# A fifth raw weight tile, adding DMAs by row blocks, a mingled step order and squares in passing tiles, in a two-layer decoder trunk

## The chip, the cores and the metric

The kernel runs on one core of one Trainium2 chip. The metric is the device time of one launch in microseconds; the time before is the median of three runs. A profile of one execution is given beside the runs.

The engines are named as in the profile: PE is TensorE (matmul), PEld its weight loads, DVE VectorE, ACT ScalarE, POOL GpSimd, SP SyncE. L12 is line 12 of the kernel.

## What is computed

The reference is a decoder trunk of two layers, D = 2048, a sequence of 256 tokens, float32. Cut to what matters:

```python
for l in range(2):
    h = rms_norm(x, attn_norm[l])
    proj = h @ w_in[l]                    # (256, 6160): columns of two head groups
    o_gla = gated linear attention        # 8 heads, chunks of 64
    o_sb = stick-breaking attention       # 8 heads, blocks of 128
    x = x + concat(o_gla, o_sb) @ w_o[l]
    hm = rms_norm(x, mlp_norm[l])
    up = square(relu(hm @ w_up[l]))       # (256, 8192)
    x = x + up @ w_down[l]
```

The change touches the last part of each layer: a rest of the input projection, the output projection, and above all the two big products of the MLP, which read 64 MB of weights each and layer.

## The kernel before

**Precision by splitting.** A float32 operand is split into a high part (its rounding to the fast matmul format, copied by ACT) and a low part (the operand less its high part, by DVE). One product of two 128-row blocks is three matmuls, high x high, high x low and low x high (L1312 to L1314); the moving side is 512 columns of weights, the stationary side 128 x 128 activations. A weight block's parts are `whi` (ACT, L1209) and `wlo` (DVE, L1213).

**Units, pairs and steps.** After the attention, a layer is a list of units: one of the gate projection ("g"), two of the output projection ("o"), then for each quarter q of the hidden width two "up" and two "down" units (n2 = 0 and 1). An up or down unit multiplies all 256 tokens with a 2048 x 1024 block of weights. It does so in eight pairs, a pair being two blocks of 128 weight rows, 1024 columns wide: one raw tile of 1 MB, loaded by one DMA on SP's queue (`load`, L1188). Four of the pairs (`FAST`, 1, 3, 5, 6) go through a Strassen-like scheme with seven products in place of eight, for which DVE first makes sums of weight blocks (`ts` and in place in `raw`, L1066); they have four steps. The others have two steps. `STEPS` lists, step by step, which pair is next; a step makes one weight operand pair of parts and then its products, into the PSUM banks that `step_banks` names.

**Adding DMAs.** For pairs 2 and 7 (`ADDED`) DVE makes no low part. ACT writes the negated high part into a tile `dlo` (L1219), and a DMA issued by POOL (L1222) adds the raw weights onto it; its landing is what the second matmul of the product waits for. A step of such a pair takes one column half (512 columns) of both row blocks, so that the DMA's source has two pieces of 2 KB in each partition.

**Rings.** Raw tiles are a ring of four (`RAWS`): three in the pool `weights`, one (`raw2`) in the pool of the MLP. A load waits until everyone who reads the tile four loads back is done, DMAs included. High parts have a ring of five, low parts one of four, `dlo` one of two. Activations (`act`, 4 KB a partition) share 19 tiles; 2 KB tiles for passing values (`t2`) are five.

**Tails.** After an up unit's last products into each bank, DVE combines the banks (`up_tail`: L1066, tile `act`), ACT applies ReLU, PE transposes the result (L1419) at the start of the next unit, ACT squares it out of PSUM (L1427) into a tile `t` of the `act` ring, and `forms` makes the parts for the down units. A down unit's tail adds the banks to the residual `xb`. The next unit's first products need the banks that the tail reads.

**The order on the queues.** `Plan` simulates the units before they are emitted: every piece has an engine, a length and a lag. PE, SP and POOL keep their order as listed; for DVE and ACT the piece that is due first goes first. What comes out is each engine's program order, and an engine that waits for one instruction holds back all behind it. Two constants tell the plan how long a transfer takes to land: 4.6 us for a load, 7.0 us for an adding DMA.

Of the kernel before, what the change touches and what calls it, by code (L numbers as in the profile page):

```python
# [20 lines left out]
T2 = 5  # L21
STEPS = [0, 0, 1, 1, 1, 1, 2, 3, 3, 2, 3, 3, 4, 4, 5, 5, 5, 5, 6, 6, 6, 6, 7, 7]
FAST = (1, 3, 5, 6)
# [20 lines left out]
class Plan:  # L44
# [10 lines left out]
    class Piece:  # L55
        def __init__(self, engine, length, fn, deps, lag):
            self.engine, self.length, self.fn, self.lag = engine, length, fn, lag
            self.deps = deps
            self.users = []
            for d in deps:  # L60
                d.users.append(self)

# [9 lines left out]

    def run(self):
        t = 0.0
        for p in self.pieces:
            if p.engine == "PE":
                p.due = t
                t += p.length
        for p in reversed(self.pieces):
            if p.engine != "PE":  # L80
                p.due = min([u.due for u in p.users], default=t) - p.length - p.lag - self.GAP
# [50 lines left out]
def trunk_kernel(  # L132
# [27 lines left out]
    xpool = ctx.enter_context(tc.tile_pool(name="resid", bufs=1, side="right"))  # L160
    apool = ctx.enter_context(tc.tile_pool(name="acts", bufs=19))
    ppool = ctx.enter_context(tc.tile_pool(name="parts", bufs=4))
# [34 lines left out]
    def tmp(tag, shape, dt=F32, bufs=2):  # L197
        pool = pools["att"] if tag in ATT else pools["mlp"] if tag in MLP else tpool
        return pool.tile(list(shape), dt, tag=tag, name=nm(tag), bufs=bufs)
# [584 lines left out]
    for l in range(DEPTH):  # L784
# [277 lines left out]
        MM, TR, V2, V1, A2, A1 = 0.227, 0.108, 1.15, 0.61, 1.0, 0.55  # L1062
        RING, LOWS, ADDS, RAWS = 5, 4, 2, 4

# [19 lines left out]

        def step_banks(kind, is_fast):

            if kind == "g":
                return (1, 6), (1, 6)
            return ((2, 3), (5, 7), (1, 6), (4,)) if is_fast else ((2, 4), (3, 8))

# [84 lines left out]
        def load(u, i):  # L1175

            box = []
            x = len(raws)

            def fn():  # L1180
                if x % 4 == 0:
                    box.append(tmp("raw2", [P, 2, 1024], bufs=1))
                else:
                    box.append(wpool.tile([P, 2, 1024], F32, tag="raw", name=nm("raw")))
                dst = box[0]
                if units[u][0] == "g":
                    dst = dst.rearrange("p k (c n) -> p (k c) n", c=2)
                nc.sync.dma_start(dst, weights(u, i))  # L1188

            readers = []  # L1190
            piece = add("SP", 2.9, fn, raws[x - RAWS] if x >= RAWS else [], lag=4.6)
            raws.append(readers)
            return (lambda: box[0]), piece, readers

        def high_tile():
# [4 lines left out]
        def parts(src, readers, deps, n=2, by_dma=False):  # L1200
# [23 lines left out]
            if by_dma:  # L1224
                m = add("ACT", A2, negated, deps, dlo[-ADDS] if len(dlo) >= ADDS else [])
                lo = add("POOL", 2.7, add_weights, m, lag=7.0)
                dlo.append([])
                readers.extend((m, lo))
# [16 lines left out]
        def steps(u, j, is_fast, r, ld, readers):  # L1245
# [17 lines left out]
            def ext(i):  # L1263
                return lambda: (op.x[j][:, i, 0, :], op.x[j][:, i, 1, :])

            if not is_fast:
                for c, ms in ((0, (2, 4)), (1, (3, 8))):
                    sl = slice(c * 512, (c + 1) * 512)
                    yield parts(
                        lambda sl=sl: r()[:, :, sl], readers, ld,  # L1270
                        by_dma=kind in ("up", "down") and j in ADDED,
                    ), [(m, [(blk(k, tt), k) for k in range(2)]) for tt, m in enumerate(ms)]
                return
            def row(k):
                return r()[:, k, :].rearrange("p (c n) -> p c n", c=2)

# [90 lines left out]
        def up_tail(u):  # L1367
# [37 lines left out]
            def turn(h):  # L1405
# [3 lines left out]

                def new_t():  # L1410
                    box["t", h] = act_tile(F32, (P, 2, 2, T))

                for i, m in enumerate(((5, 7), (1, 6))[h]):
# [10 lines left out]
                    def square(i=i):  # L1424
                        if i == 0:
                            new_t()
                        nc.scalar.activation(  # L1427
                            box["t", h][:, i].rearrange("p j t -> p (j t)"),
                            box["p", h, i], AF.Square,
                        )  # L1430
# [7 lines left out]
                    done["down", q, pair] = made(  # L1438
                        lambda i=i, pair=pair: forms(op, pair, box["t", h][:, i], "sx"),
                        None, fast(pair), sq,  # L1440
# [111 lines left out]
        for u, (kind, q, n2) in enumerate(units):  # L1552
# [4 lines left out]
            for j in order:  # L1557
                uses.append(step_banks(kind, j in quick)[of_pair[j]])
                of_pair[j] += 1
            last_use = {m: k for k, ms in enumerate(uses) for m in ms}  # L1560
            begun, p, running = set(), {}, {}
            was = units[u - 1] if u else None
            for k, j in enumerate(order):
                if j not in running:
                    running[j] = steps(u, j, j in quick, *load(u, j))
                (box, h, lo, users), prods = next(running[j])
# [78 lines left out]
```

## Time and profile before

| | |
|---|---|
| runs | 2192.98, 2190.72, 2193.82 us; median 2192.98 |
| profiled execution | 2189.26 us, of which span 2187.5 |
| granted clock of PE | 1.0 |
| PE, DVE, ACT, POOL busy | 99%, 85%, 66%, 9% of the span |
| MB moved, mean rate | 476.16 MB, 218 GB/s |

The up and down units of the first layer run from about 412 us to 1094 us, those of the second from about 1501 us to the end; the attention parts lie before them. A row of a table of windows has the stretch, its length, then for each engine the busy time and the number of instructions, the granted clock, the share of the 16 DMA engines that is busy, and GB/s. A row of the waits has who waited, for whom, the sum in us, how often, and the longest. A row of the timeline has the start, the duration, engine, line, operation, tiles and, in brackets, the idle time before it and what ended it. A row of a tile or line has the duration in ns (least, median, most) and the first and last start. In rows of DMA queues stand packets, MB and the share of 16 engines; in rows of DMA issues the KB of each and the median us to landing.

### The profile page before, as it was taken

How to read it: one execution, taken by the hardware profiler on the slowest of the kernel's cores; microseconds unless marked ns; L12 is line 12 of the kernel's file. 1: busy time of each engine (PE TensorE's matmuls, PEld its weight loads, DVE VectorE, ACT ScalarE, POOL GpSimd, SP SyncE). 2: the span in 40 equal slices, each digit the busy share in tenths (PEclk: the TensorE clock that was granted, in tenths of full speed). 3: DMA queues.
4: the chain of work that ended last, by engine and by line, in shares of the span. 5: the costliest groups of instructions: out<-in, count | busy, mean ns of one | idle time of the engine just before them, and what ended most of it. 6: DMA issues, size and time to landing. Idle time of an engine off the chain costs nothing.

```text
span 2187.5 us, 28276 instructions
## 1 busy us (share of the span) xinstructions
PE 2162.9 (99%) x10256; PEld 1781.3 (81%) x10256; DVE 1852.4 (85%) x2469; ACT 1451.4 (66%) x1855; POOL 196.1 (9%) x202
## 2 busy tenths in 40 slices
PE   9999999999999999999999999999999999999999
PEld 7988778878888888788878887788778878888887
DVE  5777569999999989999957775699899999999898
ACT  5555356677677677677745553667776776776775
POOL 0020000011010101101100200000010111111010
PEclk9999999999999999999999999999999999999999
DMA  6645455678979988888856544557888889889887
GB/s 233 194 154 159 149 175 191 211 218 254 260 231 248 254 250 234 258 255 232 224 163 193 169 158 152 175 173 217 234 250 262 229 247 262 243 239 259 250 233 212
DMA packets 179184, 476.16 MB, mean 218 GB/s; under 512 B 8698, under 2 KB 33858, under 8 KB 179044
## 3 DMA queue, kind: packets, MB, share of 16 engines
q1 hardware_dynamic: 144228, 407.24, 55.5%
q0 software_dynamic: 34816, 67.12, 18.1%
q8 instruction: 80, 1.31, 0.2%
q14 instruction: 60, 0.49, 0.1%
HBM read 405.12 MB, written 2.10 MB: 186 GB/s over the span
## 4 chain that ended last, share of the span: by engine, by line
PE 67%; DMA 14%; DVE 11%; issue 5%; ACT 1%; POOL 1%; SPq 0%; DVEq 0%; POOLq 0%; ACTq 0%
DMA dlo<-raw 7%; PE acc L557 6%; PE acc L558 6%; PE acc L559 6%; DVE wlo L1213 5%; DMA raw<-in_w_up_dram 4%; PE acc L604 3%; DMA raw<-in_w_down_dram 2%; PE acc L608 1%; DVE ts L1066 1%; DVE act L1066 1%; DVE raw L1066 1%; DVE xb L1066 1%; ACT whi L1209 1%; POOL dlo L1222 1%
## 5 line engine op out<-in xcount | busy, mean ns | idle before, releaser
L1209 ACT ACTIVATE whi<-raw 128x1024 fp32r<-128x1024 f32 (+1 forms) x728 | 701.5, 976 | 296.2 <-DVE raw L1066 45.2
L1213 DVE TENSOR_TENSOR wlo<-raw,whi 128x1024 fp32r<-128x1024 f32 (+1 forms) x600 | 654.6, 1097 | 65.8 <-ACT whi L1209 53.9
L540 DVE TENSOR_TENSOR wlo<-raw,whi 128x1024 fp32r<-128x1024 f32 (+2 forms) x194 | 220.5, 1140 | 134.0 <-ACT whi L538 133.8
L538 ACT ACTIVATE whi<-raw 128x1024 fp32r<-128x1024 f32 (+2 forms) x194 | 189.8, 983 | 203.8 <-PE acc L559 154.2
L1222 POOL DMA_DIRECT2D dlo<-raw x128 | 154.7, 1267 | 1502.4 <-ACT dlo L1219 1211.1
L557 PE MATMUL acc<-whi,act 128*128 128x512 f32 (+2 forms) x640 | 242.3, 379 | 0.0
L558 PE MATMUL acc<-wlo,act 128*128 128x512 f32 (+2 forms) x640 | 237.3, 371 | 0.0
L559 PE MATMUL acc<-whi,act 128*128 128x512 f32 (+2 forms) x640 | 236.7, 370 | 0.0
L1066 DVE TENSOR_TENSOR ts<-raw 128x1024 f32<-128x1024 f32 x136 | 165.6, 1218 | 24.6 <-DMA raw<-in_w_up_dram 22.9
L1209 ACT ACTIVATE whi<-ts 128x1024 fp32r<-128x1024 f32 x136 | 144.1, 1060 | 44.8 <-DVE ts L1066 10.7
L1219 ACT ACTIVATE dlo<-raw 128x1024 fp32r<-128x1024 f32 x128 | 130.8, 1048 | 59.0 <-DMA raw<-in_w_down_dram 35.5
L1213 DVE TENSOR_TENSOR wlo<-ts,whi 128x1024 fp32r<-128x1024 f32 x136 | 165.6, 1218 | 1.6 <-PE m__2482_12170 L1313 0.8
L557 PEld LDWEIGHTS acc<-whi,act 128*128 128x128 f32 x640 | 120.8, 189 | 22.6 <-issue 4.1
L559 PEld LDWEIGHTS acc<-whi,act 128*128 128x128 f32 x640 | 120.5, 188 | 21.1 <-issue 0.7
L558 PEld LDWEIGHTS acc<-wlo,act 128*128 128x128 f32 x640 | 120.7, 189 | 19.0 <-issue 0.7
L1066 DVE TENSOR_TENSOR raw<-raw 128x512 f32<-128x512 f32 x136 | 93.6, 688 | 2.9
L1066 DVE TENSOR_TENSOR raw<-ts,raw 128x512 f32<-128x512 f32 x136 | 92.7, 682 | 0.0
L604 PE MATMUL acc<-act,whi 128*128 128x512 f32 x256 | 91.9, 401 | 0.0
L608 PE MATMUL acc<-act,wlo 128*128 128x256 f32 x256 | 71.8, 280 | 0.0
L604 PEld LDWEIGHTS acc<-act,whi 128*128 128x128 f32 x256 | 48.1, 188 | 11.1
L1398 ACT ACTIVATE act<-act,st 128x512 f32<-128x512 f32 x64 | 41.7, 711 | 13.4 <-DVE act L1066 13.3
L608 PEld LDWEIGHTS acc<-act,wlo 128*128 128x128 f32 x256 | 48.4, 189 | 0.1
(3002 smaller groups left out, 5137.4 us busy)
## 6 DMA issues: line engine op xcount, KB each, us to landing
raw<-in_w_up_dram SPq DMA_DIRECT2D x128, 1024.0 KB, 5.1
raw<-in_w_down_dram SPq DMA_DIRECT2D x128, 1024.0 KB, 6.6
raw<-in_w_in_dram SPq DMA_DIRECT2D x84, 1024.0 KB, 5.2
dlo<-raw POOLq DMA_DIRECT2D x128, 512.0 KB, 8.8
raw<-in_w_o_dram SPq DMA_DIRECT2D x32, 1024.0 KB, 5.1
raw<-in_w_in_dram SPq DMA_DIRECT2D x14, 512.0 KB, 4.6
raw<-in_w_in_dram SPq DMA_DIRECT2D x8, 544.0 KB, 3.8
out_dram<-xb SPq DMA_DIRECT2D x8, 256.0 KB, 6.4
```

What stands on the lines that cost most here:

```text
L538: newest["hi"] = nc.scalar.activation(h, r, AF.Copy).ins
L540: newest["lo"] = nc.vector.tensor_tensor(lo[:, q : q + step, :width], r, f32(h), ALU.subtract).ins
L557: nc.tensor.matmul(o, xh[:, sl], whi[:, j, :width], start=first, stop=False)
L558: nc.tensor.matmul(o, xh[:, sl], wlo[:, j, :width], start=False, stop=False)
L559: st["mm"] = nc.tensor.matmul(o, xl[:, sl], whi[:, j, :width], start=False, stop=last).ins
L604: nc.tensor.matmul(acc[:, f, :], whi[:, j, sl], op.both(k), start=(k == 0), stop=False, skip_group_check=True,)
L608: nc.tensor.matmul(acc[:, f, T:], wlo[:, j, sl], xh, start=False, stop=(k == KT - 1), skip_group_check=True,)
L1066: nc.vector.tensor_tensor(dst, a, b, op)
L1209: nc.scalar.activation(box["h"][:, :n], src(), AF.Copy)
L1213: nc.vector.tensor_tensor(box["l"][:, :n], src(), f32(box["h"][:, :n]), ALU.subtract)
L1219: nc.scalar.activation(box["l"], src(), AF.Copy, scale=-1.0)
L1222: nc.gpsimd.dma_start(f32(box["l"]), src(), accum_op=ALU.add)
```

## The change

- `RAWS` is 5: `raw2` has two tiles. The `act` ring has 17 tiles in place of 19.
- The squares of an up unit go to tiles of 2 KB (`t2`) that are shared with other passing values, in place of `act` tiles of their own.
- Pair 2's steps take one block of 128 rows each with all 1024 columns (4 KB in a row of a partition) in place of a column half of both blocks; each of its steps then feeds four banks. Pair 7, the last of a unit, keeps its steps by column halves, but its raw tile is loaded by two DMAs, one for each column half, so that a half lies in one piece of 4 KB.
- `STEPS` is another order: pair 2's first step comes before pair 1's last, pair 6's first before pair 5's last two.
- All loads of a unit are listed at its start (in the same order), and what they wait for is filled in later (`after`), so the plan sorts its pieces before it works out when each is due.
- The plan reckons with 7.0 us for a load and 6.0 us for an adding DMA.

```diff
--- before.py
+++ after.py
@@ -19,7 +19,8 @@
 EPS = 1e-6
 WARM0, WARM1 = 8, 6
 T2 = 5
-STEPS = [0, 0, 1, 1, 1, 1, 2, 3, 3, 2, 3, 3, 4, 4, 5, 5, 5, 5, 6, 6, 6, 6, 7, 7]
+STEPS = [0, 0, 1, 1, 1, 2, 3, 1, 3, 2, 3, 3, 4, 4, 5, 5, 6, 5, 5, 6, 6, 6, 7, 7]
+LOADS = [0, 1, 2, 3, 4, 5, 6, 7]
 FAST = (1, 3, 5, 6)
 ADDED = (2, 7)
 DEPTH = 2
@@ -57,8 +58,7 @@
             self.engine, self.length, self.fn, self.lag = engine, length, fn, lag
             self.deps = deps
             self.users = []
-            for d in deps:
-                d.users.append(self)
+            self.after = []
 
     def __init__(self):
         self.pieces = []
@@ -71,12 +71,24 @@
         return self.pieces[-1]
 
     def run(self):
+        for p in self.pieces:
+            p.deps = p.deps + p.after
+            for d in p.deps:
+                d.users.append(p)
         t = 0.0
         for p in self.pieces:
             if p.engine == "PE":
                 p.due = t
                 t += p.length
-        for p in reversed(self.pieces):
+        wait = {p: len(p.deps) for p in self.pieces}
+        topo = [p for p in self.pieces if not p.deps]
+        for p in topo:
+            for u in p.users:
+                wait[u] -= 1
+                if not wait[u]:
+                    topo.append(u)
+        assert len(topo) == len(self.pieces)
+        for p in reversed(topo):
             if p.engine != "PE":
                 p.due = min([u.due for u in p.users], default=t) - p.length - p.lag - self.GAP
         line = {e: [p for p in self.pieces if p.engine == e] for e in ("PE", "SP", "POOL")}
@@ -158,7 +170,7 @@
 
     cpool = ctx.enter_context(tc.tile_pool(name="const", bufs=1, side="right"))
     xpool = ctx.enter_context(tc.tile_pool(name="resid", bufs=1, side="right"))
-    apool = ctx.enter_context(tc.tile_pool(name="acts", bufs=19))
+    apool = ctx.enter_context(tc.tile_pool(name="acts", bufs=17))
     ppool = ctx.enter_context(tc.tile_pool(name="parts", bufs=4))
     wpool = ctx.enter_context(tc.tile_pool(name="weights", bufs=3, side="right"))
     tpool = ctx.enter_context(tc.tile_pool(name="temps", bufs=2, side="right"))
@@ -1060,7 +1072,9 @@
         plan = Plan()
         add = plan.add
         MM, TR, V2, V1, A2, A1 = 0.227, 0.108, 1.15, 0.61, 1.0, 0.55
-        RING, LOWS, ADDS, RAWS = 5, 4, 2, 4
+        RING, LOWS, ADDS, RAWS = 5, 4, 2, 5
+        LAND = 7.0
+        ADD = 6.0
 
         def combine(dst, a, b, op=ALU.add):
             nc.vector.tensor_tensor(dst, a, b, op)
@@ -1082,10 +1096,13 @@
                 return [j for j in pairs for _ in range(4 if j < 2 else 2)], (0, 1)
             return STEPS, FAST
 
-        def step_banks(kind, is_fast):
-
+        def step_banks(u, j, is_fast):
+
+            kind = units[u][0]
             if kind == "g":
                 return (1, 6), (1, 6)
+            if kind in ("up", "down") and j in ADDED and not by_columns(u, j):
+                return ((2, 4, 3, 8),) * 2
             return ((2, 3), (5, 7), (1, 6), (4,)) if is_fast else ((2, 4), (3, 8))
 
         banks = {}
@@ -1178,19 +1195,32 @@
             x = len(raws)
 
             def fn():
-                if x % 4 == 0:
-                    box.append(tmp("raw2", [P, 2, 1024], bufs=1))
+                if x % RAWS in (0, 2):
+                    box.append(tmp("raw2", [P, 2, 1024], bufs=2))
                 else:
                     box.append(wpool.tile([P, 2, 1024], F32, tag="raw", name=nm("raw")))
-                dst = box[0]
+                dst, src = box[0], weights(u, i)
                 if units[u][0] == "g":
                     dst = dst.rearrange("p k (c n) -> p (k c) n", c=2)
-                nc.sync.dma_start(dst, weights(u, i))
+                if by_columns(u, i):
+                    for c in range(2):
+                        nc.sync.dma_start(
+                            dst[:, c, :].rearrange("p (k n) -> p k n", k=2),
+                            src[:, :, c * 512 : (c + 1) * 512],
+                        )
+                else:
+                    nc.sync.dma_start(dst, src)
 
             readers = []
-            piece = add("SP", 2.9, fn, raws[x - RAWS] if x >= RAWS else [], lag=4.6)
+            piece = add("SP", 2.9, fn, lag=LAND)
+            if x >= RAWS:
+                piece.after = raws[x - RAWS]
             raws.append(readers)
             return (lambda: box[0]), piece, readers
+
+        def by_columns(u, i):
+
+            return units[u][0] in ("up", "down") and i in ADDED and i == unit_order(u)[0][-1]
 
         def high_tile():
             if len(whi) % RING == 0:
@@ -1223,7 +1253,7 @@
 
             if by_dma:
                 m = add("ACT", A2, negated, deps, dlo[-ADDS] if len(dlo) >= ADDS else [])
-                lo = add("POOL", 2.7, add_weights, m, lag=7.0)
+                lo = add("POOL", 2.7, add_weights, m, lag=ADD)
                 dlo.append([])
                 readers.extend((m, lo))
             h = add("ACT", A2 if n == 2 else A1, high, deps, whi[-RING], last.get("h"))
@@ -1263,16 +1293,26 @@
             def ext(i):
                 return lambda: (op.x[j][:, i, 0, :], op.x[j][:, i, 1, :])
 
+            def row(k):
+                return r()[:, k, :].rearrange("p (c n) -> p c n", c=2)
+
             if not is_fast:
+                added = kind in ("up", "down") and j in ADDED
+                if added and not by_columns(u, j):
+                    for k in range(2):
+                        yield parts(lambda k=k: row(k), readers, ld, by_dma=True), [
+                            (m, [(blk(k, tt), c)])
+                            for c, ms in enumerate(((2, 4), (3, 8)))
+                            for tt, m in enumerate(ms)
+                        ]
+                    return
                 for c, ms in ((0, (2, 4)), (1, (3, 8))):
                     sl = slice(c * 512, (c + 1) * 512)
                     yield parts(
-                        lambda sl=sl: r()[:, :, sl], readers, ld,
-                        by_dma=kind in ("up", "down") and j in ADDED,
+                        (lambda c=c: row(c)) if added else (lambda sl=sl: r()[:, :, sl]),
+                        readers, ld, by_dma=added,
                     ), [(m, [(blk(k, tt), k) for k in range(2)]) for tt, m in enumerate(ms)]
                 return
-            def row(k):
-                return r()[:, k, :].rearrange("p (c n) -> p c n", c=2)
 
             def w(k, c):
                 return lambda: r()[:, k, c * 512 : (c + 1) * 512]
@@ -1407,9 +1447,6 @@
                 _, q, n2 = units[u]
                 op = up.setdefault(q, Operand())
 
-                def new_t():
-                    box["t", h] = act_tile(F32, (P, 2, 2, T))
-
                 for i, m in enumerate(((5, 7), (1, 6))[h]):
                     def turn_one(i=i, m=m):
                         pt = box["p", h, i] = bank(m)
@@ -1422,10 +1459,9 @@
                                 )
 
                     def square(i=i):
-                        if i == 0:
-                            new_t()
+                        box["t", h, i] = tmp("t2", [P, 2, T], bufs=T2)
                         nc.scalar.activation(
-                            box["t", h][:, i].rearrange("p j t -> p (j t)"),
+                            box["t", h, i].rearrange("p j t -> p (j t)"),
                             box["p", h, i], AF.Square,
                         )
 
@@ -1436,7 +1472,7 @@
                     pair = 4 * n2 + 2 * h + i
 
                     done["down", q, pair] = made(
-                        lambda i=i, pair=pair: forms(op, pair, box["t", h][:, i], "sx"),
+                        lambda i=i, pair=pair: forms(op, pair, box["t", h, i], "sx"),
                         None, fast(pair), sq,
                     )
 
@@ -1555,14 +1591,16 @@
                 tails[u] = (up_tail if kind == "up" else down_tail)(u)
             of_pair, uses = {j: 0 for j in order}, []
             for j in order:
-                uses.append(step_banks(kind, j in quick)[of_pair[j]])
+                uses.append(step_banks(u, j, j in quick)[of_pair[j]])
                 of_pair[j] += 1
             last_use = {m: k for k, ms in enumerate(uses) for m in ms}
             begun, p, running = set(), {}, {}
             was = units[u - 1] if u else None
+            loads = LOADS if kind in ("up", "down") else list(dict.fromkeys(order))
+            raw = {j: load(u, j) for j in loads}
             for k, j in enumerate(order):
                 if j not in running:
-                    running[j] = steps(u, j, j in quick, *load(u, j))
+                    running[j] = steps(u, j, j in quick, *raw[j])
                 (box, h, lo, users), prods = next(running[j])
                 ready = done.get((kind, q, j))
                 for m, blocks in prods:
```

## The prediction

> **What bounds the kernel now.** I read the page first, then the table of windows, the waits by engine, and the timeline around the longest waits.
>
> ```profile
> span 2187.5 us, 28276 instructions
> PE 2162.9 (99%) x10256; PEld 1781.3 (81%) x10256; DVE 1852.4 (85%) x2469; ACT 1451.4 (66%) x1855; POOL 196.1 (9%) x202
> q1 hardware_dynamic: 144228, 407.24, 55.5%
> q0 software_dynamic: 34816, 67.12, 18.1%
> 412.00:1094.00 682.00, 674.37 (x3032) 553.43 (x3031) 632.91 (x805) 502.96 (x607) 77.89 (x70) 1.00 0.86 243
> 1501.00:2180.00 679.00, 672.10 (x3013) 551.44 (x3012) 630.91 (x799) 495.64 (x589) 75.02 (x63) 1.00 0.86 243
> 1845.10:1886.10 41.00, 40.92 (x181) 33.59 (x180) 36.16 (x42) 27.86 (x31) 5.08 (x5) 1.00 0.92 274
> ```
>
> TensorE is the bound: 99% busy, at the full granted clock. The change touches the two stretches of up and down units (16 units each, rows five and six), and there the other engines are near their limits too: VectorE 632.91 of 682 us (93%), the DMA engines 0.86. The last row is an undisturbed unit: 180 products in 41.0 us, 0.228 us each. The number of products does not change, so all that can be won is time in which TensorE waits. It is idle for 682.00 - 674.37 = 7.6 us and 679.00 - 672.10 = 6.9 us, 14.5 us together. That is a lower bound, since a matmul is drawn longer than the step from one to the next:
>
> ```profile
> 879.47 0.39 PE L1314 MATMUL m__1508_7394<-whi,act 128*128 128x512 f32 x1
> 879.69 0.39 PE L1312 MATMUL m__1514_7421<-whi,act 128*128 128x512 f32 x1
> 881.41 0.50 PE L1313 MATMUL m__1514_7421<-dlo,act 128*128 128x512 f32 x1 [1.33 <-DMA dlo<-raw]
> 881.74 0.40 PE L1314 MATMUL m__1514_7421<-whi,act 128*128 128x512 f32 x1
> 454.45 0.39 PE L1314 MATMUL m__733_3754<-whi,act 128*128 128x512 f32 x1
> 456.88 0.47 PE L1312 MATMUL m__806_4097<-whi,act 128*128 128x512 f32 x1 [2.04 <-DVE act L1066]
> PE m__2741_13486 L1312 <- DVE act L1066: 2.0, 1, 2.0
> PE m__3050_14937 L1312 <- DVE act L1066: 0.2, 1, 0.2
> PE m__1514_7421 L1313 <- DMA dlo<-raw: 1.3, 1, 1.3
> PE m__3832_18608 L1313 <- DMA dlo<-raw: 0.3, 1, 0.3
>   DMA dlo<-raw: 20.8, 31
> ```
>
> Undisturbed starts are 0.22 to 0.23 apart (879.47 to 879.69) while each matmul shows 0.39, so every wait hides 0.39 - 0.23 = 0.16 us more, and the matmul after it comes 0.33 - 0.23 = 0.1 us late (881.41 to 881.74).
>
> There are two kinds of wait. The first is in the last step of a unit: the product waits for an adding DMA (dlo). The tile's row counts 31 idle times: nine of matmuls, 1.3 us down to 0.3 (first and last are shown), 6.0 in sum, and so 22 of weight loads with 14.8 us. A weight load that waits also shows the lead it should have had, some 0.25 us, so the delay is 14.8 - 22 x 0.25 = 9.3 us. Taking starts apart as above I find 20 of them in last steps with 8.8 us, and 20 x 0.1 = 2.0 behind them. **Term A: 10.8 us.** The second kind is in the first step of a unit: the bank is not free, because VectorE has not finished the former unit's tail. Two such waits are of 2.0 us; seven behind the tail of an up unit are listed, the last with 0.2 us, and three of 0.2 us behind that of a down unit. With the hidden part and those too short for the list, by starts: 9.1 + 1.6 us, and some 0.8 us behind them. **Term B: 11.5 us.** A and B are 22.3 us, which agrees with 14.5 us idle, 36 waits x 0.16 = 5.8, and 2.0 behind the adds.
>
> Who makes VectorE late? Its timeline before the wait at 456.88, and the chain of waits for the same place:
>
> ```profile
> 450.25 1.23 DVE L1066 TENSOR_TENSOR ts<-raw 128x1024 f32<-128x1024 f32 x1 [3.04 <-DMA raw<-in_w_up_dram]
> 454.92 1.21 DVE L1213 TENSOR_TENSOR wlo<-raw,whi 128x1024 fp32r<-128x1024 f32 x1
> 456.05 0.68 DVE L1066 TENSOR_TENSOR act<-m__720_3699,act 128x512 f32<-128x512 f32 x1
> 440.48 9.74 DMA raw<-in_w_up_dram
> DVE ts L1066 <- DMA raw<-in_w_up_dram: 12.0, 4, 3.5
> ACT dlo L1219 <- DMA raw<-in_w_down_dram: 18.4, 6, 3.7
> SPq L1188 <- DVE wlo L1213: 428.6, 76, 12.4
> SPq L1188 <- DMA dlo<-raw: 109.1, 30, 6.8
> ```
>
> The queue stands 3.04 us in front of a weight sum whose raw tile has not landed; the add that frees the bank (m__720, 456.05) stands seven instructions behind it. TensorE's 2.04 us are less than those 3.04. The four waits for w_up in the first stretch (12.0 us) are before the four up-to-up borders; ScalarE loses 18.4 us in the same way to w_down. The loads start late: SyncE waits 428.6 us for VectorE to read a raw tile, and 109.1 us, 30 times, for an adding DMA that still reads one. So both terms have the depth of the raw ring behind them.
>
> **The change part by part.**
>
> Five raw tiles. A load now waits for the readers of the tile five loads back, not four. A unit has eight pairs in 41.0 us, so it may start some 5.1 us earlier. Needed are 3.0 to 3.5 us for VectorE and at most 3.7 for ScalarE, so by these rows the waits for raw go. With the new step list it is more: pair 7's load waits for pair 2 (steps 5 and 9) and not for pair 3 (last at 11), and the load for pair 1 of the next unit for pair 4 (13) and not pair 5 (17). What limits a gain is the DMA engines' load.
>
> Row blocks. An add of pair 2 or 7 now moves a contiguous 4 KB per partition, not two pieces of 2 KB. Where the adds collide with loads:
>
> ```profile
> q0 software_dynamic: 544, 1.05, 47.2%
> q1 hardware_dynamic: 536, 2.08, 40.2%
> DMA to landing us min/median/max: 5.8/9.0/12.2
> dlo<-raw POOLq DMA_DIRECT2D x128, 512.0 KB, 8.8
> raw<-in_w_in_dram SPq DMA_DIRECT2D x14, 512.0 KB, 4.6
> L1188 SPq DMA_DIRECT2D raw<-in_w_down_dram x2: 367/368/368, 479.1 to 486.0; - x2
> ```
>
> The first three rows are of the window 484 to 498, with the two adds of one pair 7 and loads beside them. The adds hold each engine 0.472 x 14 = 6.6 us for 544 / 16 = 34 packets, 0.19 us a packet; a load's packet takes 0.402 x 14000 / 33.5 = 168 ns for twice the bytes. If add and load packets take turns, two adds take 6.6 + 34 x 0.168 = 12.3 us, which is the 12.2 of the slower landing. With half as many, larger packets: 6.6 + 17 x 0.168 = 9.5 us if the time goes by bytes, 3.3 + 2.9 = 6.2 us if it goes by packets. I take the byte end, since a load's packet is of that kind: 2.7 us earlier; the other end is 6 us. Term A's longest wait is 1.72 - 0.23 = 1.5 us. If an engine gave each queue longer turns, say 16 packets, the length of a row would change nothing and this gain is 0; but then the second of two adds would be through after 3.3 + 16 x 0.168 + 3.3 = 9.3 us, and the slower landing shows 12.2.
>
> The Trainium skill (DMA: Bandwidth & Descriptors, Queues, rings and completion order) says just that: an engine switches queues only after a whole packet of typically 9 to 17 descriptors. By that rule an add is a single turn before and after, and the row blocks bring nothing; by the rows above they bring 2.7 us. The landing of 12.2 us speaks for the rows, and no 4 KB add has been seen yet.
>
> Pair 7's load in two column halves: 32 more SyncE issues (one a unit) of 0.37 us, 12 us on a queue that waits 428.6 us in one layer; counted at nothing. Each half is 512 KB; such loads land in 4.6 us, so the first half comes no later than a whole tile, the second 0 to 4.6 us later. Its cover are the 5.1 us above; without them term A comes back.
>
> Mingled steps, squares, fewer act tiles:
>
> ```profile
> 501.71 1.19 POOL L1222 DMA_DIRECT2D dlo<-raw  x1 [15.25 <-ACT dlo L1219]
> L1313 PE MATMUL m__890_4484<-dlo,act x2: 389/389/389, 512.4 to 513.1; 128*128 128x512 f32 x2
> L1427 ACT ACTIVATE act<-m__1440_7068 x1: 582/582/582, 805.2 to 805.2; 128x512 f32<-128x512 f32 x1
> L434 DVE TENSOR_TENSOR act<-act,act 128x512 fp32r<-128x512 f32 x64 | 43.7, 682 | 0.0
> 150.00:200.00 50.00, 50.00 (x289) 43.53 (x288) 33.47 (x44) 26.51 (x37) 0.61 (x2) 1.00 0.56 170
> ```
>
> Pair 2's first step moves from 6 to 5, ahead of pair 1's last (three products, 0.68 us), so its two ACT copies, its POOL issue (1.2 us) and its add are due 0.7 us sooner; pair 2's raw tile now comes earlier by more than that. Today its first add is issued at 501.71 and used at 512.4: 10.7 us, less 8.8 us median landing, leaves 1.9 us. POOL has nothing else queued there. Pair 1's last step moves from 5 to 7, and pair 6's first from 18 to 16, ahead of pair 5's last two: no instruction is added, but VectorE's 1.22 + 0.68 + 1.22 us for pair 6 come sooner, before two products' worth of pair 5. Today no product inside a unit waits for wlo beyond 0.1 us, so I count 0; if VectorE's lead (four wlo tiles) were used up, it would cost up to one 1.22 us piece a unit, 32 x 1.22 = 39 us.
>
> The squares go to five small buffers shared with others instead of the act ring. The instruction (0.58 us) is the same. A fourth square may have to wait for a buffer until a low part of an earlier pair is done (0.68 us), with ScalarE's queue behind it; the bank that it frees is wanted two or three steps later, some 5 us. Cost 0; without that cover 16 up units x 0.68 = 11 us. Seventeen act tiles instead of nineteen: the attention part has TensorE busy without a gap (50.00 of 50 us); a wait there would be POOL's or VectorE's for a tile, counted at 0, at most 2 us for the two layers. The plan's new constants (LAND, ADD) only order the pieces.
>
> The sum against the profiled execution: 2189.26 us (span 2187.5 and 1.8 around it) - 10.8 (A) - 11.5 (B) + 3 for waits that come next in a VectorE that stays 93% busy (I take a quarter of B) = 2170.0. The median of the runs, 2192.98, is 3.7 above that execution; on its scale **2173.5 us**, 0.9% less. Bounds: everything within units that is not product spacing (another 6 us of 0.1 us delays) also gone, 2193 - 22.3 - 6 = 2165; only A gone and a few new delays, 2187.
>
> **The rivals.**
>
> 1. Slower: pair 2's adds become the wait. SyncE no longer holds loads back, so loads run beside the adds of pair 2 as they do now beside those of pair 7, and its first add lands like a contested one, 12.2 us after issue instead of 8.8. Against 1.9 - 0.7 = 1.2 us of slack that is 12.2 - 8.8 - 1.2 = 2.2 us of waiting in each of 32 units, 70 us, less the 22 of A and B: 2193 + 48 = 2241. It decides from 1.2 + 22.3 / 32 = 1.9 us of later landing on. For it: DMA engines at 0.86 already. Against it: pair 2's load and hence its issue come some 5 us sooner, and its adds have half the packets. The Trainium skill (DMA: Bandwidth & Descriptors, Issuing engines are not separate DMA queues) says that DMAs of all issuing engines run on the same 16 engines and interleave; the window 484 to 498 agrees, with 47.2% and 40.2% of the same engines. That is the rule that speaks against starting loads earlier.
>
> 2. Half of it: the DMA engines are too full for loads to come sooner. A goes by the row blocks alone (2.7 us against at most 1.5), VectorE still waits 3 us for raw, and B stays: 2193 - 10.8 = 2182.
>
> 3. The change does nothing that can be measured: turns are long, so that rows of 4 KB bring 0, and the loads come no sooner, so that A's and B's waits stay as they are. 2193.
>
> **How the numbers follow.** Both terms mostly gone (2167 to 2180): 0.62. Rival 2 (2180 to 2187): 0.16. Better than that: 0.03. Rival 3 (2188.6 to 2197.4; 0.2%, 4.4 us, is what a measurement of this kernel can tell from no change): 0.09, of which 0.03 for the long turns. Rival 1, small or large: 0.10. So faster 0.81, same 0.09, slower 0.10. The range reaches from 2165 to 2187 and leaves out rivals 1 and 3, 0.19.
>
> **What would show it.** In the profile after: the idle times until "DMA dlo<-raw" fall from 31 to a few, and in none is it a matmul of 1 us; VectorE's "ts" waits for raw no longer show 3 us; TensorE's idle in the two stretches falls from 14.5 to under 4 us; SyncE's wait for dlo moves from pair 3's load to pair 4's. The adds land under 8 us in the median. Wrong would be: dlo waits at step 5 of the units (rival 1), VectorE waits for raw as long as before (rival 2), or new waits of TensorE for wlo in steps 16 to 21, where pairs 5 and 6 are mingled.

## The result, and the profile after

The median of five runs is 2174.09 us (2173.94 to 2175.34), against 2190.72 (2189.61 to 2193.82) for five runs of the kernel before: a ratio of 0.9923, interval 0.9908 to 0.9937. The forecast was 2173.5, in a range of 2165 to 2187. The profiled execution took 2175.34 us.

The page after, in the rows that answer those of before, and two groups that count later:

```profile
span 2173.2 us, 28234 instructions
PE 2159.4 (99%) x10256; PEld 1784.1 (82%) x10256; DVE 1857.4 (85%) x2469; ACT 1456.6 (67%) x1855; POOL 152.0 (7%) x202
q1 hardware_dynamic: 152932, 407.24, 54.8%
q0 software_dynamic: 18432, 67.12, 16.4%
L1252 POOL DMA_DIRECT2D dlo<-raw x128 | 110.3, 862 | 1531.3 <-ACT dlo L1249 862.8
L1080 DVE TENSOR_TENSOR ts<-raw 128x1024 f32<-128x1024 f32 x136 | 166.2, 1222 | 2.4
dlo<-raw POOLq DMA_DIRECT2D x128, 512.0 KB, 5.2
```

The work is the same: as many instructions on every computing engine, as many MB. The adds make 18432 packets in place of 34816, POOL spends 862 ns on an issue in the mean where it was 1267, and an add lands after 5.2 us in the median (8.8 before). VectorE's weight sums (`ts`) had idle times of 3 us ahead of them; now all 136 have 2.4 us.

The table of windows, for the same two stretches (the second ends at 2168, since the run is shorter):

```profile
412.00:1094.00 682.00, 679.95 (x3069) 561.05 (x3067) 645.73 (x820) 511.20 (x619) 60.42 (x76) 1.00 0.82 245
1501.00:2168.00 667.00, 663.81 (x2980) 547.36 (x2979) 628.12 (x793) 492.22 (x577) 53.29 (x62) 1.00 0.81 243
```

TensorE is idle for 2.05 and 3.19 us, 5.2 together, where it was 14.5. What is left, from the waits of TensorE and of SyncE's queue; the third row is TensorE at the start of the next layer, and the fourth is the same place in the kernel before:

```profile
PE m__3867_18681 L1353 <- DMA dlo<-raw: 1.2, 1, 1.2
PE m__897_4500 L1352 <- DVE act L1080: 0.3, 1, 0.3
PE ps L461 <- DVE xb L1080: 0.2, 1, 0.2
PE ps L449 <- DVE xb L1066: 2.7, 3, 1.8
SPq L1212 <- DVE wlo L1243: 1286.6, 218, 14.2
SPq L1207 <- DMA dlo<-raw: 16.6, 6, 10.3
SPq L1212 <- DMA dlo<-raw: 1.9, 2, 1.3
```

Of the nine matmuls that waited for an adding DMA one is left: step 5 of the very last unit, where out stores run beside the adds. The loads hardly wait for an adding DMA any more (16.6 + 1.9 us). The row of 0.3 us for `act` is one of 14 such rows, one for each of 14 unit borders. The timeline at one of them:

```profile
834.36 0.68 DVE L1080 TENSOR_TENSOR act<-m__1456_7114,act 128x512 f32<-128x512 f32 x1
834.96 1.22 DVE L1243 TENSOR_TENSOR wlo<-raw,whi 128x1024 fp32r<-128x1024 f32 x1
836.09 0.68 DVE L1080 TENSOR_TENSOR act<-m__1434_7019,act 128x512 f32<-128x512 f32 x1
836.92 0.47 PE L1352 MATMUL m__1521_7412<-whi,act 128*128 128x512 f32 x1 [0.29 <-DVE act L1080]
```

VectorE is not late because of a transfer here: it works without a gap. A 1.22 us low part stands in its program order ahead of the add that frees the bank (834.96 before 836.09). By starts of matmuls each of these 14 costs 0.45 us.

### The profile page after: what moved, and what is told of

The parts are those of the page before. It is cut to its first block, busy times and chain, and to the rows that moved or that the text cites. A ratio compares the mean times of both kernels' runs of the same rounds, so it can differ in the third digit from the quotient of the medians.

```text
span 2173.2 us, 28234 instructions
## 1 busy us (share of the span) xinstructions
PE 2159.4 (99%) x10256; PEld 1784.1 (82%) x10256; DVE 1857.4 (85%) x2469; ACT 1456.6 (67%) x1855; POOL 152.0 (7%) x202
## 3 DMA queue, kind: packets, MB, share of 16 engines
q0 software_dynamic: 18432, 67.12, 16.4%
## 4 chain that ended last, share of the span: by engine, by line
PE 92%; DVE 4%; issue 2%; ACT 1%; DMA 1%; SPq 0%; POOL 0%; ACTq 0%
PE acc L569 6%; PE acc L571 6%; PE acc L570 6%; PE acc L616 3%; DVE act L1080 2%; PE acc L620 1%; DVE wlo L1243 1%; ACT whi L1239 1%; PE ps L1037 1%; PE ps L1049 1%; DMA dlo<-raw 1%; DVE t L1080 0%; PE ps L996 0%; PE ps L732 0%; PE ps L678 0%
## 5 line engine op out<-in xcount | busy, mean ns | idle before, releaser
L1239 ACT ACTIVATE whi<-raw 128x1024 fp32r<-128x1024 f32 x728 | 704.5, 978 | 299.4 <-ACT dlo L1249 29.3
L1243 DVE TENSOR_TENSOR wlo<-raw,whi 128x1024 fp32r<-128x1024 f32 x600 | 653.6, 1099 | 64.8 <-ACT whi L1239 55.9
L1252 POOL DMA_DIRECT2D dlo<-raw x128 | 110.3, 862 | 1531.3 <-ACT dlo L1249 862.8
L446 DVE TENSOR_TENSOR act<-t,act 128x512 fp32r<-128x512 f32 x76 | 52.0, 685 | 0.0
```

Source lines behind the costliest of these rows:

```text
L1239: nc.scalar.activation(box["h"][:, :n], src(), AF.Copy)
L1243: nc.vector.tensor_tensor(box["l"][:, :n], src(), f32(box["h"][:, :n]), ALU.subtract)
L1252: nc.gpsimd.dma_start(f32(box["l"]), src(), accum_op=ALU.add)
```

## The experiments

Ratios are to the kernel before, run on the same chip beside each kernel, with 95% intervals.

**One part at a time.** Row blocks alone: the kernel before with the new `step_banks`, `by_columns` and `steps`, a ring of four and the old order of steps.

```diff
+            if kind in ("up", "down") and j in ADDED and not by_columns(u, j):
+                return ((2, 4, 3, 8),) * 2
...
+                    for k in range(2):
+                        yield parts(lambda k=k: row(k), readers, ld, by_dma=True), [
```

> The kernel before with the row blocks alone (4 KB rows in the adds, pair 7's raw tile loaded in two column halves); ring of four, old step order, old places of the squares. Theory (the last-step waits come from the adds' landing, the first-step waits from the depth of the raw ring): the adds land in 5 to 6 us in the median instead of 8.8, TensorE's waits for dlo in last steps are gone (10.8 us), VectorE still waits 2 to 3.5 us for raw tiles and the waits in first steps stay: ratio 0.995, some 2181 us. Rival (the ring of five does everything, row length nothing): dlo waits as before, ratio 1.000.

Measured: 2182.84 us, 0.9969 (0.9956 to 0.9981). No matmul waits for an adding DMA; VectorE still waits for raw tiles. The DMA queues of the same 14 us, 484 to 498, that the prediction showed of before (two adds of one pair 7, loads beside them), and two rows of waits:

```profile
q1 hardware_dynamic: 663, 2.58, 45.9%
q0 software_dynamic: 288, 1.05, 45.7%
DMA to landing us min/median/max: 4.6/6.6/8.6
DVE ts L1066 <- DMA raw<-in_w_up_dram: 18.6, 8, 2.8
SPq L1198 <- DMA dlo<-raw: 76.9, 41, 4.9
```

The adds hold an engine for 0.457 x 14 = 6.4 us with 288 / 16 = 18 packets, 355 ns each, where it was 194 ns: 1.8 times the time for twice the bytes. The slower add lands after 8.6 us, not 12.2, beside more loads (2.58 MB for 2.08). It is no single case: in 35 places two adds are issued within 1.6 us, and the second lands after 8.6 us in the median, 12.0 in the kernel before. Row blocks take the first kind of wait away by themselves, and leave the second: by starts the first-step delays are 13.3 us (10.7 before), so that some 7 us show in the time and not the 10.8 of the theory.

Five raw tiles alone (with what makes room for the fifth: squares in `t2`, 17 `act` tiles).

```diff
-        RING, LOWS, ADDS, RAWS = 5, 4, 2, 4
+        RING, LOWS, ADDS, RAWS = 5, 4, 2, 5
-                if x % 4 == 0:
-                    box.append(tmp("raw2", [P, 2, 1024], bufs=1))
+                if x % RAWS in (0, 2):
+                    box.append(tmp("raw2", [P, 2, 1024], bufs=2))
...
-    apool = ctx.enter_context(tc.tile_pool(name="acts", bufs=19))
+    apool = ctx.enter_context(tc.tile_pool(name="acts", bufs=17))
...
+                        box["t", h, i] = tmp("t2", [P, 2, T], bufs=T2)
```

> The kernel before with five raw tiles (and the squares in 2 KB tiles and 17 act tiles, which make the room); adds in 2 KB pieces, old step order, plan with old lags. Theory: VectorE's and ScalarE's waits for raw go, first-step waits of TensorE shrink to 0.45 us each, and the adds start 5 us sooner, so the dlo waits in last steps go too although an add still takes 8 to 9 us: ratio 0.993, some 2175 us. Rival (row blocks are needed; the DMA engines are too full for loads to come sooner): dlo waits stay, ratio 0.997 to 1.000.

Measured: 2174.18 us, 0.9929 (0.9916 to 0.9941), the whole of the change's gain. From its tile and wait rows:

```profile
  DMA dlo<-raw: 3.7, 2
DMA to landing us min/median/max: 5.0/6.3/14.5
SPq L1188 <- DMA dlo<-raw: 148.5, 55, 8.4
```

The adds still move two pieces of 2 KB, but the tile shows 2 idle times for them where there were 31, and VectorE waits for no raw tile. Two-piece adds land after 6.3 us in the median here and 8.8 in the kernel before, so part of the landing was when the add was issued and beside which loads. The loads still wait for adds 55 times (148.5 us), and nothing comes of it.

The new order of steps alone, in the kernel before (the old `STEPS` line replaced by the new one):

> The kernel before with the new step order alone (ring of four, 2 KB pieces, old lags). The changed kernel with its ring back at four was 2.4% slower, with 50 us of dlo waits in last steps and step 5. Theory (the mingled order delays the load of pair 5, which with four tiles waits for pair 1's last step, now 7 and not 5, and all loads behind it on the queue): 30 to 60 us slower here too, ratio 1.015 to 1.03, with dlo waits. Rival (the plan's lags or the row blocks did it): ratio 1.000 within 0.003.

Measured: 2183.85 us, 0.9976 (0.9967 to 0.9985). The theory that the order needs the fifth tile fell: alone it brings 0.24%. From its tile:

```profile
  DMA dlo<-raw: 3.0, 3
DMA to landing us min/median/max: 5.0/6.3/12.2
```

So the order alone takes the waits for adds away too, with pieces of 2 KB and four tiles. By starts it leaves 12.5 us of first-step delays.

**One part taken out of the change.** Adds in 2 KB pieces again, pair 7 loaded whole:

```diff
-            if kind in ("up", "down") and j in ADDED and not by_columns(u, j):
-                return ((2, 4, 3, 8),) * 2
...
-            return units[u][0] in ("up", "down") and i in ADDED and i == unit_order(u)[0][-1]
+            return False
...
```

> The changed kernel with the adds in 2 KB pieces again (pair 2 by column halves, pair 7's raw tile loaded by one DMA). Theory: the adds' packets go back to 0.18 to 0.19 us for 2 KB, landing to 7 to 9 us, but they start early enough: few dlo waits, ratio 0.993. Rival (with five tiles loads run beside the adds, so they land at 11 us and pair 2's step 5 or pair 7's steps wait): dlo waits of 10 us or more in sum, ratio 0.997 or above.

Measured: 2175.92 us, 0.9935 (0.9923 to 0.9947). With five tiles the row blocks are worth some 0.1%, which the intervals do not tell from nothing, and what shows is the last unit's wait for an add, 2.6 us in place of 1.2.

The old order of steps in the changed kernel:

> The changed kernel with the old step order. Theory (with five tiles the order is worth nothing, as the ring alone already gave 0.993): ratio 0.992 to 0.993. Rival (mingling evens out VectorE's work and is worth some 0.1 to 0.3%): ratio 0.994 to 0.996.

Measured: 2173.14 us, 0.9930 (0.9918 to 0.9942): with five tiles the order is worth nothing that these runs can tell.

A ring of four in the changed kernel (all else as in the change):

```diff
-        RING, LOWS, ADDS, RAWS = 5, 4, 2, 5
+        RING, LOWS, ADDS, RAWS = 5, 4, 2, 4
...
```

> The changed kernel with the raw ring back at four tiles, all else of the change kept. Theory: VectorE waits for raw tiles again (20 us in the up and down units), first-step waits of TensorE come back to some 10 us, dlo waits stay away: ratio 0.995 to 0.996, some 2181 us. Rival (the new order and lags keep VectorE from queueing in front of a late load, the ring is not needed): ratio 0.992 as the changed kernel.

Measured: 2241.96 us, 1.0235 (1.0221 to 1.0249). Both theories missed, by 60 us and more. From its waits, its tile, its timeline of ScalarE and of POOL; the last row but one is of the changed kernel, the same issue; the last is a row of the table of windows, of this kernel:

```profile
PE m__3864_18675 L1353 <- DMA dlo<-raw: 4.0, 1, 4.0
  DMA dlo<-raw: 101.8, 57
SPq L1212 <- DMA dlo<-raw: 417.2, 47, 16.3
505.92 2.01 ACT L1249 ACTIVATE dlo<-raw 128x1024 fp32r<-128x1024 f32 x2 [2.96 <-DMA raw<-in_w_down_dram]
507.27 1.80 POOL L1252 DMA_DIRECT2D dlo<-raw  x2 [16.91 <-ACT dlo L1249]
499.79 0.85 POOL L1252 DMA_DIRECT2D dlo<-raw  x1 [14.16 <-ACT dlo L1249]
676.00:679.00 3.00, 3.00 (x9) 2.32 (x9) 0.69 (x1) 1.69 (x3) 0.00 (x0) 0.56 0.83 242
```

SyncE holds loads back 417 us for adding DMAs (219 in the kernel before); so pair 2's raw tile comes late, ScalarE waits 2.96 us for it, and its add is issued at 507.27, 5.6 us after its unit began (the changed kernel: 499.79, 0.6 us before). By starts TensorE loses 34.9 us in 20 last steps and 13.8 us in 7 units at step 5. Adds themselves land after 6.2 us in the median: they are issued late, they are not slow. The clock takes some 10 us more: behind six waits of 2.3 to 4.1 us, though not behind every wait of that length, the granted clock falls to about half for some 3.4 us or longer (0.56 in the row shown), and 48 matmuls of the two stretches come 0.40 to 0.45 us apart, not 0.23. The kernel has row blocks and the new order, which gain when alone, so something else in the change costs much as soon as the fifth tile is missing.

**What costs with four tiles.** Left over are the two together, the listing of loads at a unit's start, and the plan's two constants. First, row blocks and the new order in the kernel before:

> The kernel before with row blocks and the new step order, ring of four, lags of before (4.6 us for a load, 7.0 for an add). It and the next two look for what made the changed kernel with a ring of four 2.35% slower, since row blocks alone gained 0.3% and the order alone 0.2%. Theory (the plan's new lags: told that an add takes 6 us and a load 7, the plan puts ScalarE's negated copies late, and with four tiles the next load waits for the add): no trouble here, ratio 0.994 to 0.998. Rival (rows and order together, pair 2 then holds its raw tile too long): ratio 1.02.

Measured: 2182.99 us, 0.9970 (0.9958 to 0.9981). No harm, and no more than row blocks alone. Then the same with the constants of the change:

```diff
-            piece = add("SP", 2.9, fn, raws[x - RAWS] if x >= RAWS else [], lag=4.6)
+            piece = add("SP", 2.9, fn, raws[x - RAWS] if x >= RAWS else [], lag=7.0)
-                lo = add("POOL", 2.7, add_weights, m, lag=7.0)
+                lo = add("POOL", 2.7, add_weights, m, lag=6.0)
```

> As the run beside it, with the new lags (7.0 us for a load, 6.0 us for an add); against the changed kernel with four tiles only the place of the squares, the act ring of 19 and the listing of the loads differ. Theory (lags): ratio 1.015 to 1.025, with dlo waits of some 50 us. Rival (squares in 2 KB tiles or 17 act tiles): ratio below 1.000.

Measured: 2242.21 us, 1.0237 (1.0220 to 1.0255), the slow time again. And the constants alone, in the kernel before:

> The kernel before with nothing but the new lags in its plan. Theory (lags are to blame by themselves): ratio above 1.01. Rival (only together with rows and order, where pair 2's first step comes sooner): ratio within 0.005 of 1.

Measured: 2217.59 us, 1.0120 (1.0101 to 1.0139). From its tile:

```profile
  DMA dlo<-raw: 82.4, 74
DMA to landing us min/median/max: 5.0/7.5/12.7
```

74 idle times until an add where there were 31, though adds land sooner than before (7.5 against 8.8 us). Two numbers that no instruction carries cost 1.2%, and 2.4% together with row blocks and order. Which of the two does it was not tried.

**The wait that is left.** The plan takes one event at a time and picks an engine's next piece at once. Where the piece that frees a bank becomes ready at the same moment, but is taken from the list later, a low part that is due later is picked first. The edit takes all events of a moment before it picks:

```diff
                     came.add(p)
                 count += 1
+            if events and events[0][0] <= now + 1e-9:
+                continue
```

In the changed kernel:

> The changed kernel, with one thing altered in the plan's simulation: all events of the same moment are taken in before an engine chooses its next piece. In the changed kernel VectorE takes a wlo of 1.22 us between the tail's last sum and the add that frees the first bank, because that add becomes ready in the very moment in which the engine chooses. Theory (this tie makes the 14 waits of 0.45 us in first steps): the add comes first, those waits and the 0.1 us behind them go, 8 us: ratio 0.9885 to 0.9895. Rival (VectorE is at 95% and simply late; the wlo that moves back is then waited for): ratio 0.992 to 0.993.

Measured: 2161.01 us, 0.9873 (0.9860 to 0.9887), the fastest kernel here; the changed kernel with the old order, in the same set of runs, took 2173.14. The first stretch moved to 405 to 1084, first of the changed kernel, then of this one, and all of this kernel's waits of TensorE that the view lists:

```profile
405.00:1084.00 679.00, 676.99 (x3055) 558.83 (x3054) 643.21 (x815) 509.68 (x614) 58.83 (x72) 1.00 0.83 247
405.00:1084.00 679.00, 679.00 (x3077) 564.04 (x3076) 648.30 (x821) 506.61 (x617) 60.16 (x74) 1.00 0.86 248
PE ps L521 <- POOL ident masks.py:199: 1.5, 1, 1.5
PE ps L463 <- DMA xb<-in_x_dram: 1.3, 2, 1.1
PE ps L680 <- DVE act L645: 0.4, 2, 0.2
PE m__2488_12189 L1355 <- DVE wlo L1245: 0.3, 1, 0.3
```

TensorE is busy 679.00 of 679.00 us, and at no unit border is a wait left. The gain is more than the 8 us of the theory: by starts all 8.9 us at the unit borders went, the last unit's wait for an add too (1.4 us), and in this execution the first up unit began 2.7 us sooner than in that of the changed kernel, which these traces do not explain. VectorE at the same border as above:

```profile
827.91 0.68 DVE L1082 TENSOR_TENSOR act<-m__1432_7018,act 128x512 f32<-128x512 f32 x1
828.51 0.68 DVE L1082 TENSOR_TENSOR act<-m__1456_7114,t 128x512 f32<-128x512 f32 x1
829.11 0.68 DVE L1082 TENSOR_TENSOR act<-m__1434_7030,act 128x512 f32<-128x512 f32 x1
829.71 1.22 DVE L1245 TENSOR_TENSOR wlo<-raw,whi 128x1024 fp32r<-128x1024 f32 x1
```

The adds that free banks now stand ahead of the low part.

The same in the kernel with only the ring of five:

> The kernel with the ring of five alone, and the plan's ties resolved as in the run beside it. Theory: ring and ties are all there is to win; as fast as the changed kernel with the ties resolved, ratio 0.9885 to 0.990. Rival (row blocks or mingling matter once the border waits are gone): 0.2% or more slower than that one.

Measured: 2162.70 us, 0.9881 (0.9868 to 0.9895): row blocks, order and constants add nothing that these runs can tell. And in the kernel before:

> The kernel before with the plan's ties resolved as in the fastest run so far, ring of four. Theory (with four tiles VectorE queues in front of late loads whatever the order at the border, so the ties are worth little before the ring is deeper): ratio 0.998 to 1.000. Rival (the tie is worth its 0.6% by itself): ratio 0.994.

Measured: 2179.58 us, 0.9955 (0.9940 to 0.9970), nearer to the rival than to the theory: the tie costs 0.45% with four tiles as well, where a wait for a raw tile had been the only cause that I saw. From its waits and its tile:

```profile
DVE ts L1068 <- DMA raw<-in_w_up_dram: 19.5, 8, 4.1
DMA to landing us min/median/max: 5.1/9.1/14.6
```

VectorE still waits up to 4.1 us for raw tiles, and adds land no sooner than before (9.1 us, 8.8 before). Yet by starts the delays in first steps fall from 13.0 us to 4.3, those in last steps from 10.9 to 1.8, each with what follows them; some 7 us come anew, most of it in waits for low parts at step 5. The edit reorders the whole of both queues, so the borders' share is not taken apart.

## Why the prediction was right, and where not

**The place and the size.** The gain is in TensorE's waits in up and down units, as forecast, and the time came out within a microsecond of the sum. Its terms did not, and that the two agree so well is luck.

**Term A** (10.8 us) held: the 20 last-step delays of 8.8 us and what follows them are gone, less 1.3 us plus what follows for the new one in the last unit. It was put down to two causes, and either is enough: row blocks alone end it with four tiles, five tiles alone with 2 KB pieces, but for the last unit. The new order alone nearly does as well, and so does the plan without its tie, whose adds land no sooner; when an add is issued matters, not only how long it takes. So the gains do not add: 0.31%, 0.71% and 0.24% for the three parts alone, 0.77% for all.

**Term B** (11.5 us) was mis-sized, with its allowance of 3 us for what comes next. VectorE no longer waits for raw tiles, and the waits of 2.0 us went; but by starts the first-step delays went from 9.1 + 1.6 us only to 6.3 + 0.9, and what follows them stayed, some 0.8 us. Of B only some 3.5 us came, so waits that stayed or came anew cost 8.0 us and not 3. The prediction named "a VectorE that stays 93% busy" as their cause. The runs showed another: the tie in the plan, which puts a low part ahead of the freeing add. With the tie out and VectorE busier still (648.30 of 679 us, 95%), no such wait is left. The failed step is the reading that all of the delay at a bank came from the 3 us in front of the late tile; the order of the seven instructions behind it was left out, though the prediction's own rows show the same low part (454.92) directly ahead of the freeing add (456.05).

**What made up for it.** For the profiled execution the sum said 2170.0 us; it took 2175.34, so 13.9 us were gained and not 19.3. A brought 9.4, B 3.5, and 2.5 came at the border of the layers, which the prediction did not count: TensorE's waits there (2.7 us) fell to 0.2. Against it, the first up unit began 2.7 us later (412.07 and 414.74 us) in this execution; why, these runs do not settle. Some 1 us is not accounted for. The rest is the scale. The prediction added 3.7 us to go from its execution to the median of three runs, but the median of five is only 1.5 us above that execution, and the changed kernel's profiled execution is 1.25 us above its own median. Between the medians the gain is 16.6 us, where 19.5 was forecast.

**Row blocks.** The byte end (a packet of 4 KB takes nearly twice one of 2 KB) held: 355 against 194 ns in the shown window, and over the whole run 0.164 x 16 x 2173.2 / 18432 = 309 ns against 0.181 x 16 x 2187.5 / 34816 = 182. What failed is that add and load packets take turns one by one. From the same window, the kernel before at 485 to 489 (first row) and at 489.5 to 492 (the next two), then row blocks alone at 489 to 492.5:

```profile
q0 software_dynamic: 247, 0.51, 89.1%
q1 hardware_dynamic: 184, 0.75, 90.5%
q0 software_dynamic: 2, 0.00, 0.1%
q0 software_dynamic: 104, 0.43, 76.0%
q1 hardware_dynamic: 97, 0.40, 30.1%
```

In the kernel before the first add ran alone, then a load alone, then the second add, as the next load began. These are the long turns that the prediction set aside since they gave 9.3 us and not 12.2; but a landing counts from the issue, some 1.5 us before the first packet for the first add (484.04 and about 485.5), and the three transfers took 4 to 4.5 us each where 3.3, 2.7 and 3.3 were reckoned. So these rows fit the rule that the prediction weighed (the Trainium skill, DMA: Bandwidth & Descriptors, Queues, rings and completion order: an engine changes queues only after a packet of many descriptors). The rows of the row blocks do not: there the second add and the load ran side by side. The landing, which by the prediction's use of that rule would have stayed, came 3.6 us sooner, and not 2.7. Why larger pieces mix more finely is not shown, and not all do: the second of two adds still lands after more than 9 us in 10 of the 35 places (33 before).

**What was counted at nothing.** The new order, the squares with the 17 `act` tiles and the 32 more issues cost nothing that can be seen in the whole with five tiles. "The plan's new constants only order the pieces" holds, as far as tried, only with five tiles: with four they cost 27 us alone, and 59 us on top of row blocks and order (2182.99 to 2242.21). The sum did not need it, but no bound was given for it, and it is the largest price in this study. Squares and fewer `act` tiles were tried apart from the fifth tile only with the listing of loads, and cost nothing there: 2241.96 us with the three, 2242.21 without.

**Rivals.** Rival 1 put 2241 us on a kernel whose pair-2 adds become the wait. It did not happen; but the kernel with a ring of four has waits at step 5 and 2242 us. Its mechanism is not the rival's: more is lost in last steps (34.9 us) than at step 5 (13.8), the adds land after 6.2 us, and are issued late because the loads before them are held back. Rival 2 (2182, row blocks without sooner loads) is what row blocks alone measured, 2182.84. Rival 3 fell: its long turns are there in the kernel before, but rows of 4 KB brought the adds forward all the same.

**The signs named.** dlo waits from 31 idle times to a few, no weight sum behind a 3 us wait, adds under 8 us: as named. Two missed: TensorE's idle in the stretches is 5.2 us, not under 4; and SyncE's wait for adds did not move to pair 4's load, it all but vanished. "In none is it a matmul of 1 us" missed by the last unit's 1.2 us.

## What to carry to other kernels

When two causes can each remove a wait, test them one by one: here one more buffer in the load ring did all that three reworked parts did together. Where program order comes from a simulated schedule, its constants and its ties are part of the kernel: when an engine without a gap still delays another, look at the order of the instructions just ahead of the one that is awaited. A constant that is harmless in one version should be measured again when a buffer is taken away.

## What the chip showed that was not expected

- An adding DMA's packet goes nearly by bytes (182 ns for 2 KB pieces, 309 ns for 4 KB over a run, 355 ns in a crowded window), but an issue by POOL with half as many pieces takes 0.86 us in place of 1.2 us.
- Two adds and a load at the same time went one whole transfer after another with pieces of 2 KB, and in part side by side with pieces of 4 KB.
- The same two-piece adds land after 8.8 us in the median with four raw tiles, 7.5 us with other constants, 6.3 us with the new order or with five tiles: a good part of a landing time was company, not size. In the changed kernel's last unit, with out stores beside the adds, the landing reaches the largest of the run:

```profile
DMA to landing us min/median/max: 4.5/5.2/11.7
```
